# Two pairs of RWKV chunks share one triangular solve, each row on two partitions, all steps on VectorE

## The chip, the cores and the metric

The kernel runs on one core of one Trainium2 chip. A core has TensorE (PE: matmuls and transposes), VectorE (DVE), ScalarE (ACT), GpSimd (POOL) and SyncE (SP, which starts the transfers), each with a queue of its own that it works off in order. The metric is the device time of one execution in microseconds (us); less is better. The time before is 3129.33 us, the median of 3 runs (3124.56 to 3129.62).

## The reference

Two layers (DEPTH = 2) work on 512 latent tokens and 256 context tokens of width 1024. Each layer is a SwiGLU block, a mixer and a second SwiGLU block. The mixer projects its input once, gives a quarter of the width each to attention, RWKV-7 in both directions, pooling and a Fourier transform, and projects the four together back (`w_out`). The change lies in the RWKV part, whose core is a recurrence over time, for 4 heads of 64 and both directions:

```python
def wkv_scan(S0, r, w, k, v, a, b, reverse, emit):
    def step(S, inp):
        r_t, w_t, k_t, v_t, a_t, b_t = inp
        sa = jnp.einsum('bhvk,bhk->bhv', S, a_t)
        S = S * w_t[:, :, None, :] + sa[..., None] * b_t[:, :, None, :] + v_t[..., None] * k_t[:, :, None, :]
        y = jnp.einsum('bhvk,bhk->bhv', S, r_t) if emit else None
        return S, y

    xs = tuple(jnp.moveaxis(t.astype(F32), 1, 0) for t in (r, w, k, v, a, b))
    S_final, ys = lax.scan(step, S0, xs, reverse=reverse)
    return (jnp.moveaxis(ys, 0, 1) if emit else None), S_final
```

The context is scanned first, and its final states are the initial ones of the latent scan. Attention (softmax over 768 keys for the latent tokens) does not depend on the recurrence and is worked off beside it.

## The kernel before

Everything runs under a tile framework: the code names tiles and engines, the framework orders each engine's queue by the order of the code and by priority (`with hot():` lifts what stands in it ahead of other work), and it puts in the waits. Tiles come from pools of fixed size; the solve takes its scratch M and Xs from the pool "w" (11 slots), which also holds the weight tiles.

The recurrence is worked in chunks of 64 tokens. Both directions run at the same time on the two halves of the partitions. There are three groups per mixer: C (the 256 context tokens), L0 (latent, offsets 0 and 256) and L1 (offsets 256 and 0); a group has two pairs of chunks, so a mixer has 12 chunks. Per pair there are three stages:

- `group_pair` scales keys, values and decays (VectorE, GpSimd) into AR and BK, and multiplies them into the chunk's "gram" blocks (line 952, masked at 956). From these comes NTX (line 960), the strictly triangular matrices whose inverses (I + N) are wanted: 32x32 blocks, for 4 heads, 2 directions, 2 chunks and both halves of each chunk, 32 blocks in a pair.
- `group_solve` inverts them. M is the matrix with one block on each partition (line 998 and 1001 transposes, 999 and 1000 copies). X starts as the identity and is worked in 31 steps, j = 31 down to 1, each a multiplication (line 1011) and an addition (line 1013). Each block has four partitions, with 8 of its 32 rows on each. These steps run on GpSimd, except in the first pair of L1 ("late"), where VectorE has them. Behind them stand copies and transposes (1016, 1019, 1020), a product (1030 to 1033) that fills the off-diagonal block (pm1), copies into gram (1042), a second product (1047, pm2) and the last copies (1050). From then on the pair is ready.
- `chain` goes through the pair's two chunks. Each makes z on TensorE (1068, 1071), copies it (Wz, ScalarE, line 1074), multiplies with the inverse (pu, 1077), writes UV (ScalarE 1080 and VectorE 1082), updates the state S (TensorE 1088, VectorE 1090 and 1091), and makes the output y. The next chunk needs the new S.

In the mixer's loop (1470 to 1505) C's pairs and solves come first, in `hot()`. Then both chains of C, each followed by `fill(2)`, which sends out two pieces of attention. Then for each of the four L pairs: `group_pair`, `group_solve`, `fill(2)`, and in `hot()` the chain of the pair before it. What attention is left comes after the loop, `fill(100)`. Layer 0 has 14 pieces of attention, layer 1 nine.

Of the kernel before, what the change touches and what calls it, by code (L numbers as in the profile page):

```python
# [53 lines left out]
class K:  # L54
# [856 lines left out]
    def group_pair(self, R, G, cp):  # L911
# [11 lines left out]
        H = {"G": G, "cp": cp, "gram": [], "A": A, "AR": AR, "late": s == "L" and off[0] and not cp}  # L923
# [63 lines left out]
    def group_solve(self, H):  # L987
# [3 lines left out]
        A = H["A"]  # L991
        X1T, XT, NT = A[0:32], A[32:64], A[64:96]
# [4 lines left out]
        M = w([128, 32, 32], "M")  # L997
        nc.vector.transpose(M[0:32].rearrange(fl), NT.rearrange(fl))
        nc.scalar.copy(M[32:64], M[0:32])
        nc.gpsimd.tensor_copy(M[64:96], M[0:32])  # L1000
        nc.vector.transpose(M[96:128].rearrange(fl), NT.rearrange(fl))
        XS = w([128, 1024], "Xs")
        X, tmp, Pm = XS[:, 0:256].rearrange("p (t i) -> p t i", i=32), XS[:, 256:512], XS[:, 512:768].rearrange("p (u t) -> p u t", t=32)
        nc.gpsimd.memset(XS[:, 0:256], 0.0)
        for x in range(4):
            nc.gpsimd.memset(XS[32 * x:32 * x + 32, x:256:36], 1.0)
        eng = nc.vector if H["late"] else nc.gpsimd
        for j in range(31, 0, -1):
# [18 lines left out]
        for u in range(8):  # L1027
            for d in range(2):
                r = slice(64 * d, 64 * d + 32)
                nc.tensor.matmul(p[r, u], H["gram"][d][r, u, 32:64], X1[d][:, :, 8 * d + u], start=True, stop=True)  # L1030
# [731 lines left out]
```

## Time and profile before

| | value |
|---|---|
| median of 3 runs | 3129.33 us |
| profiled execution | 3129.89 us, span 3128.1 us |
| PE, PEld busy (of the span) | 2910.2 us (93%), 2544.1 us (81%) |
| DVE, ACT, POOL busy | 2303.3 us (74%), 1313.6 us (42%), 531.4 us (17%) |
| chain that ended last | PE 73%, DVE 13%, ACT 7%, POOL 2% |

PE is the time of matmuls, PEld that of weight loads, which overlaps it. The shares are means over the whole span; most of it is SwiGLU, where TensorE is full. The two mixers' recurrences lie at about 780 to 1055 us and 2430 to 2670 us. The chain that ended last is the work followed back from the last instruction, each time to what released it.

### The profile page before, as it was taken

Reading aid. Unit: us, or ns where it says so; the run is one execution under the profiler, and the core shown is the slowest. Engines: PE = TensorE matmul, PEld = TensorE weight load, DVE = VectorE, ACT = ScalarE, POOL = GpSimd, SP = SyncE. Lnnn points to the kernel's source line nnn. Section 1 sums busy time; section 2 is a strip of 40 time slices with the busy share of each in tenths; the row PEclk is TensorE's granted clock in tenths of the full one; section 3 lists DMA queues with packets and bytes.
Section 4 is the critical chain, followed back from the end, with each engine's and each line's share of the span. In section 5 each row is a group of like instructions: output and inputs, shape, how many; then the busy total and the mean of one; then the engine's idle time right before and its main releaser. Section 6 shows DMA issues by size and latency. Waiting matters only on the chain.

```text
span 3128.1 us, 50276 instructions
## 1 busy us (share of the span) xinstructions
PE 2910.2 (93%) x20031; PEld 2544.1 (81%) x20031; DVE 2303.3 (74%) x3989; ACT 1313.6 (42%) x2208; POOL 531.4 (17%) x1117
## 2 busy tenths in 40 slices
PE   7999999999888889999998999999999897879997
PEld 5999998787555679999987999998877565679996
DVE  7879998744666768678778889777834566797887
ACT  4433332433676354333325443332433676354443
POOL 2000002103774030000022000001112764010002
PEclk8999999999686999999999999999999677889998
DMA  6334445320001213233232344434420002033332
GB/s 237 103 116 147 135 140 167 125 66 1 30 28 36 89 60 128 95 108 102 95 122 68 103 141 142 135 122 138 146 67 1 23 29 87 34 111 101 108 109 101
DMA packets 92187, 304.60 MB, mean 97 GB/s; under 512 B 13636, under 2 KB 15920, under 8 KB 91952
## 3 DMA queue, kind: packets, MB, share of 16 engines
q1 hardware_dynamic: 91952, 301.39, 29.2%
q8 instruction: 157, 2.57, 0.3%
q14 instruction: 78, 0.64, 0.1%
HBM read 279.81 MB, written 21.54 MB: 96 GB/s over the span
## 4 chain that ended last, share of the span: by engine, by line
PE 73%; DVE 13%; ACT 7%; issue 3%; DMA 2%; POOL 2%; SPq 0%; DVEq 0%; ACTq 0%; POOLq 0%
PE pab L123 8%; PE pab L124 8%; PE pab L125 8%; PE py L123 6%; PE py L124 6%; PE py L125 6%; PE pgu L123 4%; PE pgu L124 4%; PE pgu L125 4%; PE pw L123 2%; PE pw L124 2%; PE pw L125 2%; DVE wlo L119 2%; DVE raw L420 1%; PE pwo L125 1%
## 5 line engine op out<-in xcount | busy, mean ns | idle before, releaser
L118 ACT CAST whi<-raw 128x1024 fp32r<-128x1024 f32 x488 | 507.8, 1050 | 552.5 <-PE py L125 193.1
L119 DVE TENSOR_TENSOR wlo<-raw,whi 128x1024 fp32r<-128x1024 f32 x488 | 600.6, 1239 | 125.3 <-PE py L124 25.5
L123 PE MATMUL pab<-hshi,whi 128*128 128x256 f32 x1408 | 401.3, 288 | 24.5 <-ACT hshi L118 9.7
L124 PE MATMUL pab<-hslo,whi 128*128 128x256 f32 x1408 | 404.7, 288 | 8.9 <-DVE hslo L119 8.9
L125 PE MATMUL pab<-hshi,wlo 128*128 128x256 f32 x1408 | 401.8, 287 | 1.6 <-DVE wlo L119 1.5
L524 POOL TENSOR_TENSOR acc<-acc,gate 128x512 f32<-128x512 f32 x44 | 73.6, 1695 | 1631.0 <-DMA gate<-gate 1167.1
L123 PE MATMUL pab<-h,whi 128*128 128x256 f32 x1056 | 298.7, 287 | 9.7 <-DVE eab L463 7.4
L124 PE MATMUL pab<-h,whi 128*128 128x256 f32 x1056 | 301.6, 287 | 4.6 <-POOL h L317 4.5
L123 PE MATMUL pgu<-hhiC,whi 128*128 128x256 f32 x1056 | 299.7, 284 | 2.8 <-ACT h L286 2.2
L125 PE MATMUL pab<-h,wlo 128*128 128x256 f32 x1056 | 299.9, 286 | 1.9 <-DVE wlo L119 1.9
L124 PE MATMUL pgu<-hloC,whi 128*128 128x256 f32 x1056 | 299.5, 284 | 0.0
L125 PE MATMUL pgu<-hhiC,wlo 128*128 128x256 f32 x1056 | 299.1, 283 | 0.0
L123 PEld LDWEIGHTS pab<-hshi,whi 128*128 128x128 f32 x1408 | 273.3, 196 | 29.3 <-ACT hshi L118 11.2
L123 PE MATMUL py<-whi,actL 128*128 128x512 f32 x704 | 277.2, 395 | 11.0 <-DVE acc L513 8.3
L124 PEld LDWEIGHTS pab<-hslo,whi 128*128 128x128 f32 x1408 | 275.4, 196 | 11.9 <-DVE hslo L119 11.6
L125 PEld LDWEIGHTS pab<-hshi,wlo 128*128 128x128 f32 x1408 | 274.5, 196 | 3.1 <-DVE wlo L119 2.6
L124 PE MATMUL py<-wlo,actL 128*128 128x512 f32 x704 | 276.8, 393 | 0.0
L125 PE MATMUL py<-whi,actL 128*128 128x512 f32 x704 | 274.8, 391 | 0.0
L123 PEld LDWEIGHTS pab<-h,whi 128*128 128x128 f32 x1056 | 202.8, 194 | 15.9 <-DVE eab L463 8.1
L124 PEld LDWEIGHTS pab<-h,whi 128*128 128x128 f32 x1056 | 205.3, 194 | 9.3 <-POOL h L317 6.3
L125 PEld LDWEIGHTS pab<-h,wlo 128*128 128x128 f32 x1056 | 204.8, 195 | 4.1 <-DVE wlo L119 2.5
L123 PEld LDWEIGHTS pgu<-hhiC,whi 128*128 128x128 f32 x1056 | 202.8, 192 | 6.2 <-ACT h L286 2.7
(473 smaller groups left out, 6586.8 us busy)
## 6 DMA issues: line engine op xcount, KB each, us to landing
raw<-in_w_ffn_in SPq DMA_DIRECT2D x176, 512.0 KB, 3.6
rawm<-in_w_mod SPq DMA_DIRECT2D x128, 512.0 KB, 3.7
raw<-in_w_ffn_out SPq DMA_DIRECT2D x88, 512.0 KB, 3.5
raw<-in_w_in SPq DMA_DIRECT2D x24, 512.0 KB, 4.5
back<-spill SPq DMA_DIRECT2D x44, 256.0 KB, 4.3
spill<-res SPq DMA_DIRECT2D x16, 512.0 KB, 7.3
spill<-acc SPq DMA_DIRECT2D x16, 512.0 KB, 3.3
raw<-in_w_out SPq DMA_DIRECT2D x16, 512.0 KB, 3.5
```

What stands on the lines that cost most here:

```text
L118: self.nc.scalar.copy(hi, src)
L119: self.nc.vector.tensor_tensor(lo, src, hi.bitcast(F32), op=ALU.subtract)
L123: nc.tensor.matmul(out, st[0], mv[0], start=start, stop=False)
L124: nc.tensor.matmul(out, st[0], mv[1], start=False, stop=False)
L125: nc.tensor.matmul(out, st[1], mv[0], start=False, stop=stop)
L420: nc.vector.tensor_tensor(o, x, y, op=ALU.subtract)
L524: nc.gpsimd.tensor_tensor(a[:, sl], a[:, sl], self.gate[s][:, sl], op=ALU.mult)
```

## The change

`group_solve` is called once for a group, with both its pairs. The 64 blocks lie on 128 partitions, two for each block, with 16 of its 32 rows on each. The 31 steps stay, with `(16 - j//2) * j` elements per partition where it was `(8 - j//4) * j`, and their engine is VectorE in all groups. Of M, each pair's part is transposed once (before twice), and two ScalarE copies fill the other half. Copies of X and of gram halve in number and double in length; the products pm1 and pm2 stand for both pairs one behind the other. In the mixer's loop the chains of C move into the loop of L0: after each pair of a group come `fill(2)` and the chain of the group before. The solve stands behind both pairs, and the chains of L1 behind the loop. Four `fill(2)` are left of six; the rest of attention comes with `fill(100)`.

The diff, without the products and the copies into gram (the same for both pairs, in loops over `cp`):

```diff
-    def group_solve(self, H):
-
-
-        nc = self.nc
-        A = H["A"]
-        X1T, XT, NT = A[0:32], A[32:64], A[64:96]
+    def group_solve(self, Hs, eng):
+
+
+        nc = self.nc
-        M = w([128, 32, 32], "M")
-        nc.vector.transpose(M[0:32].rearrange(fl), NT.rearrange(fl))
-        nc.scalar.copy(M[32:64], M[0:32])
-        nc.gpsimd.tensor_copy(M[64:96], M[0:32])
-        nc.vector.transpose(M[96:128].rearrange(fl), NT.rearrange(fl))
+        Ms = [w([128, 32, 32], "M")]
+        M = Ms[0]
+        for cp, H in enumerate(Hs):
+            nc.vector.transpose(M[32 * cp:32 * cp + 32].rearrange(fl), H["A"][64:96].rearrange(fl))
+        nc.scalar.copy(M[64:128, 16:32], M[0:64, 16:32])
+        nc.scalar.copy(M[64:128, 0:16], M[0:64, 0:16])
...
-        X, tmp, Pm = XS[:, 0:256].rearrange("p (t i) -> p t i", i=32), XS[:, 256:512], XS[:, 512:768].rearrange("p (u t) -> p u t", t=32)
-        nc.gpsimd.memset(XS[:, 0:256], 0.0)
-        for x in range(4):
-            nc.gpsimd.memset(XS[32 * x:32 * x + 32, x:256:36], 1.0)
-        eng = nc.vector if H["late"] else nc.gpsimd
+        X, tmp = XS[:, 0:512].rearrange("p (t i) -> p t i", i=32), XS[:, 512:1024]
+        Pm = tmp.rearrange("p (c u t) -> p c u t", c=2, t=32)
+        nc.gpsimd.memset(XS[:, 0:512], 0.0)
+        for y in range(2):
+            nc.gpsimd.memset(XS[64 * y:64 * y + 64, y:512:34], 1.0)
         for j in range(31, 0, -1):
-            a = j // 4
-            tv = tmp[:, 0:(8 - a) * j].rearrange("p (t i) -> p t i", i=j)
-            eng.tensor_tensor(tv, M[:, j:j + 1, 0:j].to_broadcast([128, 8 - a, j]),
-                              X[:, a:8, j:j + 1].to_broadcast([128, 8 - a, j]), op=ALU.mult)
-            eng.tensor_tensor(X[:, a:8, 0:j], X[:, a:8, 0:j], tv, op=ALU.add)
-        for x in range(4):
-            eng = nc.scalar.copy if x % 2 else nc.gpsimd.tensor_copy
-            eng(XT[:, :, x::4], X[32 * x:32 * x + 32].rearrange("p t i -> p i t"))
-        Xb = M[0:32].rearrange("p (x t) u -> p x t u", x=4)
-        for x in range(4):
-            nc.vector.transpose(Xb[:, x].rearrange(fl), X[32 * x:32 * x + 32].rearrange(fl))
-        nc.vector.transpose(X1T.rearrange(fl), XT.rearrange(fl))
-
...
+            a = j // 2
+            tv = tmp[:, 0:(16 - a) * j].rearrange("p (t i) -> p t i", i=j)
+            eng.tensor_tensor(tv, M[:, j:j + 1, 0:j].to_broadcast([128, 16 - a, j]),
+                              X[:, a:16, j:j + 1].to_broadcast([128, 16 - a, j]), op=ALU.mult)
+            eng.tensor_tensor(X[:, a:16, 0:j], X[:, a:16, 0:j], tv, op=ALU.add)
+        Ms.append(w([128, 32, 32], "M"))
+        X1, X2, Xb = [], [], []
+        for cp, H in enumerate(Hs):
+            X1T, XT, X1T2 = [H["A"][32 * i:32 * i + 32] for i in range(3)]
+            Xc = [X[64 * y + 32 * cp:64 * y + 32 * cp + 32] for y in range(2)]
+            nc.gpsimd.tensor_copy(XT[:, :, 0::2], Xc[0].rearrange("p t i -> p i t"))
+            nc.scalar.copy(XT[:, :, 1::2], Xc[1].rearrange("p t i -> p i t"))
+            v = "p (y t) u -> p y t u"
+            Xb.append(Ms[cp][0:32].rearrange(v, y=2))
+            for y in range(2):
+                nc.vector.transpose(Xb[cp][:, y].rearrange(fl), Xc[y].rearrange(fl))
+            nc.vector.transpose(X1T.rearrange(fl), XT.rearrange(fl))
...
             g = self.group_start(P, R, "C", (0, 0), both, first)
             for cp in range(2):
                 Hs.append(self.group_pair(R, g, cp))
-                self.group_solve(Hs[cp])
+            self.group_solve(Hs, nc.vector)
...
-        prev = None
         nth = 0
-        for H in Hs:
-            with hot():
-                self.chain(R, H, False)
-            fill(FILL[l][nth])
-            nth += 1
...
+            prev, Hs = Hs, []
             g = self.group_start(P, R, s, off, em, first)
             for cp in range(2):
-                H = self.group_pair(R, g, cp)
-                self.group_solve(H)
+                Hs.append(self.group_pair(R, g, cp))
                 fill(FILL[l][nth])
                 nth += 1
-                if prev:
-                    with hot():
-                        self.chain(R, prev, False)
-                prev = H
+                with hot():
+                    self.chain(R, prev[cp], False)
+            self.group_solve(Hs, nc.vector)
...
         with hot():
+            self.chain(R, Hs[0], False)
             rw = mixes["L", 1] = self.slot([128, 2, SEQ], name="mixL")[:]
             self.rwkv_out(P, R, "L", rw, (1, 2), "rk")
-            self.chain(R, prev, True)
+            self.chain(R, Hs[1], True)
             self.rwkv_out(P, R, "L", rw, (0, 3), "rk")
         fill(100)
```

On GpSimd the first pair of L0 in layer 0 stood like this before (Xs is X and its scratch, 1011 and 1013 the steps; 1000 a copy of M):

```order
L946 TENSOR_TENSOR AR_8465<-l_r_6263,gb_8193 128x4x64
L1000 COPY M_8287<-M_8287 32x1024
L1011 TENSOR_TENSOR Xs_8292<-M_8287,Xs_8292 128x31
L1013 TENSOR_TENSOR Xs_8292<-Xs_8292 128x31
L1011 TENSOR_TENSOR Xs_8292<-M_8287,Xs_8292 128x30
L1013 TENSOR_TENSOR Xs_8292<-Xs_8292 128x30
L1011 TENSOR_TENSOR Xs_8292<-M_8287,Xs_8292 128x29
```

The new order has, at the same place:

```order
L1004 MEMSET Xs_8260 128x512
L1006 MEMSET Xs_8260 64x16 x2
L1041 MEMSET gram_8059 32x8x32
L965 MEMSET uv_8065 64x512 x2
L935 COPY AR_8529<-l_kk_6262 128x4 x2
L943 TENSOR_TENSOR AR_8529<-l_r_6263,gb_8482 128x4x64
L984 TENSOR_TENSOR kdsL_7745<-kdsL_7745,ga_8481 128x2x256
L1018 COPY NTX_7799<-Xs_8260 32x512
L1018 COPY NTX_8021<-Xs_8260 32x512
```

The 62 steps are gone; two memsets and the copies of X for both pairs (line 1018, before 1016) stand behind each other, with other work of `group_pair` between them.

On VectorE the third chunk of C in layer 0 had its update (line 1082) among attention (1228) and the gram masks (956) before:

```order
L1082 TENSOR_SCALAR uv_7422<-pch_7999 64x256
L1228 ISA pexp_8676,mx_8678<-psc_8680,zero 128x256
L1228 ISA mx_8678 128x1
L956 TENSOR_TENSOR gram_8505<-pgr_8495,prm_858_6192 128x512
L956 TENSOR_TENSOR gram_8505<-pgr_8496,prm_858_6192 128x512
L1228 ISA pexp_8675,mx_8677<-psc_8685,zero 128x512
L1228 ISA mx_8677 128x1
L998 STREAM_TRANSPOSE M_8535<-NTX_8467 32x1024
```

Now the joint solve of L0 stands around it (1010 and 1012 are the steps, 1088 is the update):

```order
L1239 RECIPROCAL mx_8813<-mx_8813 128x1
L1012 TENSOR_TENSOR Xs_8260<-Xs_8260 128x2x29
L1010 TENSOR_TENSOR Xs_8260<-M_8255,Xs_8260 128x56
L1012 TENSOR_TENSOR Xs_8260<-Xs_8260 128x2x28
L1010 TENSOR_TENSOR Xs_8260<-M_8255,Xs_8260 128x81
L1088 TENSOR_SCALAR uv_7282<-pch_8153 64x256
L1012 TENSOR_TENSOR Xs_8260<-Xs_8260 128x3x27
L1010 TENSOR_TENSOR Xs_8260<-M_8255,Xs_8260 128x78
L1012 TENSOR_TENSOR Xs_8260<-Xs_8260 128x3x26
```

What moved: the update of the third chunk comes behind nine steps of L0's solve, and 53 more follow it.

On VectorE the end of L1's second solve in layer 0 was two transposed blocks between other work, and the third chunk of L0 (uv, 1082) came behind it:

```order
L1019 STREAM_TRANSPOSE M_9489<-Xs_9494 32x256 x4
L1147 TENSOR_TENSOR mixC_7845<-mixC_7845,c_r_6257 128x256
L1020 STREAM_TRANSPOSE NTX_9419<-NTX_9419 32x1024
L1148 TENSOR_TENSOR mixC_7845<-mixC_7845,pbon_8930 128x256
L119 TENSOR_TENSOR wlo_10147<-raw_10144,whi_10146 128x1024
L1228 ISA pexp_9687,mx_9689<-psc_9691,zero 128x256
L1228 ISA mx_9689 128x1
L1082 TENSOR_SCALAR uv_8511<-pch_9315 64x256
```

Now the last steps of the joint solve of L1 stand ahead of the transposes of both pairs (1023, 1024), with weight tiles (wlo, 119) and attention (1234) behind them:

```order
L1012 TENSOR_TENSOR Xs_9034<-Xs_9034 128x15x3
L1010 TENSOR_TENSOR Xs_9034<-M_9029,Xs_9034 128x30
L1012 TENSOR_TENSOR Xs_9034<-Xs_9034 128x15x2
L1010 TENSOR_TENSOR Xs_9034<-M_9029,Xs_9034 128x16
L1012 TENSOR_TENSOR Xs_9034<-Xs_9034 128x16
L1239 RECIPROCAL mx_9613<-mx_9613 128x1
L1023 STREAM_TRANSPOSE M_9029<-Xs_9034 32x512 x2
L1023 STREAM_TRANSPOSE M_9100<-Xs_9034 32x512 x2
L1024 STREAM_TRANSPOSE NTX_8531<-NTX_8531 32x1024
L1024 STREAM_TRANSPOSE NTX_8741<-NTX_8741 32x1024
L119 TENSOR_TENSOR wlo_9823<-raw_9820,whi_9822 128x1024
```

All four chunks of L0 have their updates ahead of this place now; the first chunk of L1 has its own 17 rows further on.

## Rows read from the trace of the kernel before

**Rows 1.** Windows: us, busy PE, PEld, DVE, ACT, POOL; PEclk, DMA share, GB/s

```profile
780.00:840.00 60.00, 44.11 (x246) 31.80 (x247) 44.69 (x100) 33.97 (x95) 48.46 (x148) 0.70 0.10 39
840.00:1050.00 210.00, 177.12 (x1867) 128.75 (x1867) 132.63 (x379) 136.82 (x297) 105.03 (x312) 0.74 0.12 41
2490.00:2660.00 170.00, 143.80 (x1568) 105.56 (x1564) 109.64 (x293) 114.68 (x249) 96.77 (x292) 0.74 0.16 56
```

**Rows 2.** Groups by line, 760 to 1060 us: busy us, mean ns, idle before, releaser

```profile
L1013 POOL TENSOR_TENSOR Xs<-Xs 128x66 f32<-128x66 f32 (+22 forms) x155 | 49.9, 330 | 7.0
...
L1019 DVE STREAM_TRANSPOSE M<-Xs 32x256 f32<-32x256 f32 x24 | 10.4, 433 | 1.9 <-POOL Xs L1013 1.2
...
L1011 DVE TENSOR_TENSOR Xs<-M,Xs 128x60 f32<-128x60 f32 (+24 forms) x31 | 8.2, 263 | 0.9
L1013 DVE TENSOR_TENSOR Xs<-Xs 128x60 f32<-128x60 f32 (+24 forms) x31 | 8.1, 262 | 0.9
...
L998 DVE STREAM_TRANSPOSE M<-NTX 32x1024 f32<-32x1024 f32 x6 | 7.4, 1233 | 3.7 <-ACT NTX L960 3.6
```

**Rows 3.** Timeline of ACT, line 1074: start us, duration us, instruction, [idle before <-releaser]

```profile
844.05 0.37 ACT L1074 COPY Wz<-pch 128x256 f32<-128x256 f32 x1 [0.16 <-PE pch L1071]
...
895.80 0.36 ACT L1074 COPY Wz<-pch 128x256 f32<-128x256 f32 x1
945.17 0.37 ACT L1074 COPY Wz<-pch 128x256 f32<-128x256 f32 x1
966.69 0.37 ACT L1074 COPY Wz<-pch 128x256 f32<-128x256 f32 x1 [0.96 <-PE pch L1071]
997.31 0.37 ACT L1074 COPY Wz<-pch 128x256 f32<-128x256 f32 x1
...
1024.67 0.37 ACT L1074 COPY Wz<-pch 128x256 f32<-128x256 f32 x1
...
1048.06 0.37 ACT L1074 COPY Wz<-pch 128x256 f32<-128x256 f32 x1 [5.35 <-PE pch L1071]
...
2541.31 0.37 ACT L1074 COPY Wz<-pch 128x256 f32<-128x256 f32 x1 [1.26 <-PE pch L1071]
2561.80 0.37 ACT L1074 COPY Wz<-pch 128x256 f32<-128x256 f32 x1 [0.95 <-PE pch L1071]
2580.26 0.35 ACT L1074 COPY Wz<-pch 128x256 f32<-128x256 f32 x1
2606.37 0.37 ACT L1074 COPY Wz<-pch 128x256 f32<-128x256 f32 x1
...
2640.33 0.39 ACT L1074 COPY Wz<-pch 128x256 f32<-128x256 f32 x1
...
2667.45 0.37 ACT L1074 COPY Wz<-pch 128x256 f32<-128x256 f32 x1
```

**Rows 4.** Timeline of ACT: the second pair of L0 becomes ready (line 1050)

```profile
978.46 0.74 ACT L1050 COPY gram<-pm 32x256 f32<-32x256 f32 x2
```

**Rows 5.** Timeline of POOL: behind the first solve of C, and L0's last step

```profile
823.12 1.34 POOL L1016 COPY NTX<-Xs 32x256 f32<-32x256 f32 x2
...
946.28 0.21 POOL L1013 TENSOR_TENSOR Xs<-Xs 128x8 f32<-128x8 f32 x1
```

**Rows 6.** Timeline of DVE: the C transposition, and steps of the two late solves

```profile
803.82 1.23 DVE L998 STREAM_TRANSPOSE M<-NTX 32x1024 f32<-32x1024 f32 x1 [0.97 <-ACT NTX L960]
...
935.88 0.17 DVE L1011 TENSOR_TENSOR Xs<-M,Xs 128x31 f32<-128x31 f32 x1
...
968.42 0.37 DVE L1011 TENSOR_TENSOR Xs<-M,Xs 128x49 f32<-128x49 f32 x1
...
972.44 0.17 DVE L1011 TENSOR_TENSOR Xs<-M,Xs 128x8 f32<-128x8 f32 x1
972.65 0.17 DVE L1013 TENSOR_TENSOR Xs<-Xs 128x8 f32<-128x8 f32 x1
...
2611.27 0.21 DVE L1011 TENSOR_TENSOR Xs<-M,Xs 128x49 f32<-128x49 f32 x1
```

More of the change, by code (lines that the diff above doesn't have):

```diff
@@ L922, in group_pair @@
         mul = lambda o, a, b: nc.vector.tensor_tensor(o, a, b, op=ALU.mult)
-        H = {"G": G, "cp": cp, "gram": [], "A": A, "AR": AR, "late": s == "L" and off[0] and not cp}
+        H = {"G": G, "cp": cp, "gram": [], "A": A, "AR": AR}
         for d in range(2):
@@ L1023, in group_solve @@
-        nc.scalar.copy(X1T2[:, :, 8:16], X1T[:, :, 8:16])
-        nc.scalar.copy(M[64:96, :, 24:32], M[0:32, :, 24:32])
-        X1, X2 = (X1T, X1T2), (Xb, Xb2)
-        p = self.ps([128, 8, 32], "pm1", "sv")
-        for u in range(8):
-            for d in range(2):
-                r = slice(64 * d, 64 * d + 32)
-                nc.tensor.matmul(p[r, u], H["gram"][d][r, u, 32:64], X1[d][:, :, 8 * d + u], start=True, stop=True)
-        for d in range(2):
-            r = slice(64 * d, 64 * d + 32)
-            nc.scalar.mul(Pm[r], p[r], -1.0)
@@ L1043, in group_solve @@
-        p = self.ps([128, 8, 32], "pm2", "sv")
-        for u in range(8):
-            for d in range(2):
-                r = slice(64 * d, 64 * d + 32)
-                nc.tensor.matmul(p[r, u].rearrange("p (t x) -> p x t", x=4), Pm[r, u], X2[d][:, :, :, 16 + 8 * d + u], start=True, stop=True)
-        for d in range(2):
-            r = slice(64 * d, 64 * d + 32)
-            nc.scalar.copy(H["gram"][d][r, :, 32:64], p[r])
+        Ms = [w([128, 32, 32], "M")]
+        M = Ms[0]
+        for cp, H in enumerate(Hs):
+            nc.vector.transpose(M[32 * cp:32 * cp + 32].rearrange(fl), H["A"][64:96].rearrange(fl))
@@ new lines, in group_solve @@
+        half = [slice(64 * d, 64 * d + 32) for d in range(2)]
+        p = self.ps([128, 2, 8, 32], "pm1", "sv")
+        for cp, H in enumerate(Hs):
+            for u in range(8):
+                for d, r in enumerate(half):
+                    nc.tensor.matmul(p[r, cp, u], H["gram"][d][r, u, 32:64], X1[cp][d][:, :, 8 * d + u], start=True, stop=True)
+        for r in half:
+            nc.scalar.mul(Pm[r], p[r], -1.0)
+        for cp, H in enumerate(Hs):
+            for d in range(2):
+                gr = H["gram"][d]
+                nc.gpsimd.memset(gr[64 * d + 32:64 * d + 64, :, 0:32], 0.0)
+                for b in range(2):
+                    us = slice(16 * b + 8 * d, 16 * b + 8 * d + 8)
+                    r = slice(64 * d + 32 * b, 64 * d + 32 * b + 32)
+                    for y in range(2):
+                        cpy = nc.gpsimd.tensor_copy if y else nc.scalar.copy
+                        cpy(gr[r, :, 32 * b + y:32 * b + 32:2], Xb[cp][:, y, :, us].rearrange("p t u -> p u t"))
@@ new lines, in group_solve @@
+        p = self.ps([128, 2, 8, 32], "pm2", "sv")
+        for cp in range(2):
+            for u in range(8):
+                for d, r in enumerate(half):
+                    nc.tensor.matmul(p[r, cp, u].rearrange("p (t y) -> p y t", y=2), Pm[r, cp, u], X2[cp][d][:, :, :, 16 + 8 * d + u],
+                                     start=True, stop=True)
+        for cp, H in enumerate(Hs):
+            for d, r in enumerate(half):
+                nc.scalar.copy(H["gram"][d][r, :, 32:64], p[r, cp])
@@ L1469, in mixer @@
         mixes["L", 0] = att["L"]
[L1470 removed]
         nth = 0
[L1472 to L1476 removed]
         for s, off, em in (("L", (0, 256), True), ("L", (256, 0), True)):
[L1478 removed]
+            if off[0] == 0:
                 for n in ("kds", "Y"):
```

15 lines of the change are left out of this document (4 added, 11 removed).

## The prediction

> **What bounds the kernel now.** I read the busy time of each engine in three stretches first [rows 1]. The change touches the two mixers only, and there no engine is full: between 840 and 1050 us TensorE is busy 177.1 of 210 us, VectorE 132.6, ScalarE 136.8 and GpSimd 105.0; in the second layer TensorE has 143.8 of 170. So TensorE leaves 32.9 and 26.2 us idle, and a wait in the recurrence can be worth at most about that. The reader is to see that the stretch before it, 780 to 840, is another case: VectorE is already busy 44.7 of 60 us.
>
> Next I read the lines of the solve [rows 2]. In 760 to 1060 us GpSimd spends 49.9 us on 155 additions (five solves) and about as much on as many multiplications, VectorE 8.2 + 8.1 us on 31 of each (the one "late" solve). A GpSimd step takes 330 ns on average, a VectorE step some 262.
>
> Then I followed the recurrence by the copy that each chunk makes once (Wz, line 1074) [rows 3]. In layer 0 the four chunks of C stand 17.25 us apart on average (844.05 to 895.80). Then 49.4 us pass until the first chunk of L0 (945.17), 21.5 to its second, and 30.6 to its third (997.31). L1 begins at 1024.67 and its four chunks take 23.4 us. In layer 1 the same two waits are 20.5 us (2541.31 to 2561.80) and 26.1 (2580.26 to 2606.37). The third chunk of L0 needs the second pair, whose steps end on GpSimd at 946.28 and whose blocks are written at 978.46 [rows 4, 5]: two solves interleave on one engine there, and 32 us more pass in copies and small matmuls behind them. For the first C pair the way is shorter: steps over at 823.12 [rows 5], Wz at 844.05, 21 us.
>
> **The change part by part.** *The steps.* A joint solve is 31 steps of two operations on (16 - j//2) x j elements per partition, 2856 for each of the two, 5712 in sum. On VectorE with GpSimd idle 49 elements take 0.21 us and 8 take 0.17 [rows 6]: 1.0 ns an element over a base of 0.16, and 0.04 between two steps (972.44, the next at 972.65). So 62 x (0.16 + 0.04) + 5.7 = 18.1 us for a group. While GpSimd runs steps of its own the same 49 elements take 0.37 [rows 6]; 62 x 0.16 more makes 28 us. GpSimd has none of its steps left in the new kernel, so I take the low end, and keep 28 for the range.
>
> The Trainium skill, "SBUF — State Buffer", section "Who interferes with whom", says that VectorE and GpSimd share a pair of ports with an exclusive lock. The two prices in the group just named agree with it. It speaks for this change: it would put the steps at 18.1 us, and only GpSimd's remaining work would add to them.
>
> *VectorE's load.* The steps busy it 62 x 0.16 + 5.7 = 15.6 us a group, 47 a mixer, of which 16.3 was there [rows 2]: +31. Transposes: three of 32x1024 at 1.23 and four of 32x256 at 0.433 per pair become two of 32x1024 and two of 32x512. The last form isn't in the trace; between 0.43 and 1.23 I take 0.70 in proportion to its length. That is 5.4 to 3.9 per pair, -9 us a mixer. Net +22. Of this only about +9 falls into 840 to 1050 (two groups of 15.6, less the old 16.3 and 6 us of transposes): 132.6 becomes 141 of 210, 67%. The C group's 15.6 falls into the stretch where 44.7 of 60 are taken, and nearly fills it. GpSimd loses some 100 us; the copies that it keeps no longer stand behind steps. ScalarE's and GpSimd's strided copies halve in number and double in length; that they cost a few us more or less lies beside other work.
>
> *The C group.* The joint solve needs the second pair, whose block is transposed at 803.82 [rows 6]. 803.8 + 1.2 + 18 to 28 + 21 gives Wz at 844 to 854, before 844.05. I take +5. What hides this is TensorE's other work; if that cover is gone the whole +5 is paid. In the new order the chain of C runs beside the building of L0's pairs. At the old 17.25 us its chunks stand at 849, 866, 884 and 901.
>
> *The L0 group.* On VectorE the solve is queued behind the second C chunk's update, and the third and fourth stand inside it. These are new waits: a chunk late on TensorE holds the rest of the solve, and steps stand before a chunk's update: some 50 of the 62 between the third chunk's and the fourth's, 15 of the 18.1 us, just under the distance of the chunks, which hides them. The last step then comes at about 903; with 21 us behind it L0 begins at 924, before 945.17: -21. With the 32 us of the old second pair it would be 935, -10.
>
> *The L1 group.* Its solve starts behind L0's second chunk (924 + 21.5 = 946) and again has the two others inside: 963, 980, last step 982, L1's first chunk 1003. Before it was 1024.67: -21 holds, and no more comes in, for L0 to L1 takes 79 us as before (79.5). The old wait for the second pair (30.6) becomes a plain 17, and a new one of 23 stands before L1 instead, since both its pairs now become ready at once. By the path layer 0 thus gains 21. TensorE's cap: the 177.1 us of work in 210 can be packed, but not fully; with 8% idle it takes 192.5, a gain of 17.5. I take the smaller, **-17.5**.
>
> *Layer 1.* The first wait was only 20.5 there; 23 in its place is +2.5. L0 to L1 was 78.5 (2561.80 to 2640.33) and becomes 18.5 + 17 + 17 + 23 = 76, -2.5. The path gains nothing at the old distances. But attention moves back in the order. Of its nine pieces in this layer four stood ahead of L0's first pair and eight ahead of L1's; now it is none and four, and one stands behind the last pair. So less TensorE work stands before the solves, and more beside the L1 chain, whose 27.1 us (2640.33 to 2667.45) leave room. The cap with 8% idle is 156.3 for 170: -13.7. Between 0 and that I take **-7**.
>
> *Sum.* The profiled execution took 3129.89 us (span 3128.1), 0.6 above the median of 3129.33. 3129.9 - 17.5 - 7 = 3105.4; **3105** against the median.
>
> **The rivals.** *A, the distances shrink too.* The 17.25 us between chunks is no latency of the chain: L1's four stand 7.8 apart. With both pairs of L0 ready at once, its last two chunks and L1's start could move up by some 5 us each. That is 10 per group and layer in L0 and L1, 40 in all: 3065. For it: TensorE's weight loads fill only 128.8 of 210 us [rows 1]. Against it: attention and the next pairs still stand between these chunks.
>
> The Trainium skill, "Perfetto Trace Analysis", section "Identifying the Most-Contended Engine", calls the busy share of matmuls a bad measure of TensorE's headroom and wants that of weight loads. Here that is 61% against 84%. By it the cap falls away: layer 0 gains 21 instead of 17.5, and rival A is the case.
>
> *B, hidden.* TensorE's idle time has other causes (softmax, copies of ScalarE), and the steps' removal from GpSimd only moves the wait: 3129 within 6.
>
> *C, slower.* A joint solve delays the first pair of each group, and what comes behind the steps is done for both pairs in one piece: transposes, copies, 64 small matmuls. If that takes 32 us, as behind the old second pair, instead of 21, layer 0 has +11 twice on its -21, about 0, and layer 1 +22: 3152. Steps strung out by other VectorE work do the same; the old VectorE solve began at 935.88 and ended at 972.8 [rows 6], 37 us for 16 of work. It decides from the point where L1's last step comes later than about 1004 in layer 0 (1024.67 - 21), and 2619 in layer 1. Against it: GpSimd is free for its half of the copies.
>
> *D, no effect in the queue.* The order might have kept the solves where they were. It hasn't: the steps are gone from GpSimd's queue.
>
> **How the numbers follow.** Forecast 0.46 (3090 to 3120), A 0.18 (3055 to 3080), B 0.15 (3123 to 3135), C 0.21 (3136 to 3155), D none. The range of 8 in 10 leaves out the low half of A and some half of C: 3064 to 3143. The unknown prices lie within: solves at 28 instead of 18 us in L0 and L1 of both layers cost 40 at most, but mostly lie beside chunks that stand inside them. 0.2%, 6 us, is about what a measurement of this kernel tells from no change. Faster by more than that: forecast and A, 0.64; within: 0.15; slower: C, 0.21.
>
> **What would show it.** Steps of 0.17 to 0.25 us on VectorE, 62 for a group in 18 to 25 us of work; no steps on GpSimd. Wz of L0's first chunk near 924, of L1's near 1003; some 20 us from a last step to its group's first Wz; TensorE's idle time down in 840 to 1050. The two mixers differ in their gain, the stretches between them not at all. It would be wrong if VectorE is full from 780 to 840 and C's chain starts at 855 or later, or if the last step of L1 comes after the points above.

## The result: 3090.18 us, and the profile after

The changed kernel takes 3090.18 us in the median (3088.14 to 3093.1, 4 runs), the kernel before 3129.47 in the same comparison: a ratio of 0.9883, 95% interval 0.987 to 0.9897. That is 39 us less, 1.6 times the 24.5 that the sum gave, and at the lower edge of what was held most likely (3090 to 3120). The profiled execution took 3088.14 us, span 3086.3.

First the stages, by windows of the kernel before: layer 0 from the first matmul of the mixer's input projection to the first of its output projection (pw to pwo), the output projection, the SwiGLU blocks between, the next input projection from 4 us behind its start to the second pwo, and that output projection (the 39 us between the third and the fourth are left out). Columns as in [rows 1].

```profile
642.00:1053.60 411.60, 359.76 (x2879) 273.41 (x2877) 238.18 (x619) 222.21 (x484) 175.84 (x480) 0.82 0.11 37
1053.60:1138.60 85.00, 79.16 (x354) 63.70 (x355) 59.40 (x129) 31.85 (x47) 14.54 (x16) 0.96 0.19 69
1138.60:2259.60 1121.00, 1087.92 (x7435) 1010.63 (x7434) 875.23 (x1312) 403.84 (x597) 76.58 (x57) 0.98 0.35 115
2299.00:2668.00 369.00, 320.72 (x2478) 240.60 (x2476) 204.78 (x514) 202.13 (x425) 162.87 (x472) 0.79 0.13 43
2668.00:2730.00 62.00, 53.77 (x249) 41.12 (x249) 40.57 (x92) 17.46 (x24) 5.04 (x5) 0.92 0.08 26
```

The same five stages of the changed kernel:

```profile
641.30:1026.20 384.90, 345.91 (x2854) 263.02 (x2853) 246.80 (x720) 210.73 (x447) 67.57 (x112) 0.84 0.10 34
1026.20:1108.90 82.70, 78.74 (x378) 62.95 (x379) 60.25 (x133) 33.00 (x49) 16.11 (x17) 1.00 0.28 99
1108.90:2225.30 1116.40, 1085.64 (x7435) 1008.98 (x7434) 875.10 (x1312) 404.26 (x597) 76.72 (x57) 0.99 0.35 115
2265.00:2631.70 366.70, 307.21 (x2492) 232.99 (x2490) 224.37 (x621) 191.69 (x388) 59.70 (x105) 0.81 0.12 43
2631.70:2687.60 55.90, 51.71 (x233) 40.11 (x232) 40.04 (x91) 17.41 (x24) 6.09 (x5) 0.95 0.09 29
```

Layer 0 gives 26.7 us up to pwo and 2.3 in it; layer 1 gives 2.3 and 6.1; the blocks between 4.6, though nothing in them was changed. The reader should look at TensorE's two parts. In layer 0 its idle time falls from 51.8 to 39.0 us, and its busy time from 359.8 to 345.9 (25 of some 2870 records fewer lie in that stretch, worth about 3 us at the mean). In layer 1 the idle time *rises* from 48.3 to 59.5, and the busy time falls from 320.7 to 307.2, though 14 matmuls more lie there. Over the whole span the page counts the same 20031 matmuls in both kernels:

```profile
PE 2910.2 (93%) x20031; PEld 2544.1 (81%) x20031; DVE 2303.3 (74%) x3989; ACT 1313.6 (42%) x2208; POOL 531.4 (17%) x1117
```

is the page before, and

```profile
PE 2877.6 (93%) x20031; PEld 2522.9 (82%) x20031; DVE 2332.7 (76%) x4201; ACT 1292.8 (42%) x2136; POOL 322.4 (10%) x383
```

after. Of the 41.8 us of span 32.6 are TensorE's own busy time, 9.2 its idle time. The mean granted clock went from 0.931 to 0.941 of the full 2.4 GHz, and 2910.2 x 0.931 / 0.941 is 2879.3, close to the 2877.6 measured.

The recurrence, by the copy Wz of its chunks as in [rows 3] (the line is 1080 now), with the copies that make L0 ready (1056):

```profile
852.27 0.37 ACT L1080 COPY Wz<-pch 128x256 f32<-128x256 f32 x1
889.84 0.37 ACT L1080 COPY Wz<-pch 128x256 f32<-128x256 f32 x1 [1.43 <-PE pch L1077]
926.38 1.49 ACT L1056 COPY gram<-pm 32x256 f32<-32x256 f32 x4
931.12 0.37 ACT L1080 COPY Wz<-pch 128x256 f32<-128x256 f32 x1
962.13 0.37 ACT L1080 COPY Wz<-pch 128x256 f32<-128x256 f32 x1
998.82 0.36 ACT L1080 COPY Wz<-pch 128x256 f32<-128x256 f32 x1
1024.83 0.37 ACT L1080 COPY Wz<-pch 128x256 f32<-128x256 f32 x1 [1.92 <-PE pch L1077]
...
2464.73 0.37 ACT L1080 COPY Wz<-pch 128x256 f32<-128x256 f32 x1
2533.24 0.37 ACT L1080 COPY Wz<-pch 128x256 f32<-128x256 f32 x1
2600.32 0.37 ACT L1080 COPY Wz<-pch 128x256 f32<-128x256 f32 x1
2628.05 0.37 ACT L1080 COPY Wz<-pch 128x256 f32<-128x256 f32 x1 [0.75 <-PE pch L1077]
```

These are the first and last chunk of each group in layer 0, and in layer 1 the first of each group and the last of all. L0 begins at 931.12 instead of 945.17, L1 at 998.82 instead of 1024.67, and the last chunk comes at 1024.83 instead of 1048.06. C's chunks stand 12.5 us apart (17.25 before), L0's 10.3.

The solves in windows from first to last step: C, L0 and L1 of layer 0. Columns as above.

```profile
799.50:827.30 27.80, 25.34 (x112) 18.48 (x112) 23.07 (x102) 14.26 (x42) 0.19 (x1) 0.88 0.20 78
874.20:898.10 23.90, 19.70 (x168) 14.87 (x166) 20.48 (x75) 14.11 (x29) 2.23 (x2) 0.71 0.01 2
946.10:975.10 29.00, 24.23 (x303) 16.22 (x301) 25.60 (x105) 19.15 (x43) 0.00 (x0) 0.99 0.00 1
```

The same windows, only VectorE's instructions on the tile Xs (columns: us, VectorE busy and count, clock, DMA share, GB/s):

```profile
799.50:827.30 27.80, 15.71 (x62) 0.88 0.20 78
874.20:898.10 23.90, 16.38 (x63) 0.71 0.01 2
946.10:975.10 29.00, 15.67 (x62) 0.99 0.00 1
```

The 62 steps take 15.7 us in C and L1, as worked out, and 16.4 in L0 (the 63rd instruction there is a transposition). But a solve lasts 24 to 29 us in layer 0, and 24, 32 and 31 in layer 1: in its stretch in layer 0 VectorE is busy 83 to 88%, with 4 to 10 us of other work between the steps. The steps' own work follows what GpSimd does meanwhile: over the six solves it is 15.7 to 15.8 us where GpSimd is busy up to 0.2 us, 16.4 and 16.8 where it is busy 2.2 and 2.4, and 18.2 where it is busy 4.8 (the second of layer 1). Such a place in L0, VectorE's timeline, where two updates of the state (1096, 1097) stand among steps:

```profile
880.97 0.29 DVE L1010 TENSOR_TENSOR Xs<-M,Xs 128x126 f32<-128x126 f32 x1
881.64 0.87 DVE L1096 TENSOR_TENSOR S<-prm,pch 64x256 f32<-64x256 f32 x2 [0.38 <-PE pch L1094]
882.54 0.29 DVE L1012 TENSOR_TENSOR Xs<-Xs 128x126 f32<-128x126 f32 x1
882.75 0.86 DVE L1097 TENSOR_TENSOR S<-S,PC 64x256 f32<-64x256 f32 x2
```

### The profile page after: what moved, and what is told of

Its sections match the earlier page's. It is cut to its first block, busy times and chain, and to the rows that moved or that the text cites. A ratio compares the mean times of both kernels' runs of the same rounds, so it can differ in the third digit from the quotient of the medians.

```text
span 3086.3 us, 49684 instructions
## 1 busy us (share of the span) xinstructions
PE 2877.6 (93%) x20031; PEld 2522.9 (82%) x20031; DVE 2332.7 (76%) x4201; ACT 1292.8 (42%) x2136; POOL 322.4 (10%) x383
## 5 line engine op out<-in xcount | busy, mean ns | idle before, releaser
L118 ACT CAST whi<-raw 128x1024 fp32r<-128x1024 f32 x488 | 507.9, 1050 | 535.7 <-PE py L125 177.2
L123 PE MATMUL pab<-hshi,whi 128*128 128x256 f32 x1408 | 400.8, 288 | 25.4 <-ACT hshi L118 10.3
L123 PEld LDWEIGHTS pab<-hshi,whi 128*128 128x128 f32 x1408 | 272.7, 195 | 30.0 <-ACT hshi L118 11.6
L124 PEld LDWEIGHTS pab<-hslo,whi 128*128 128x128 f32 x1408 | 275.2, 196 | 11.9 <-DVE hslo L119 11.6
```

What stands on the lines that cost most here:

```text
L118: self.nc.scalar.copy(hi, src)
L123: nc.tensor.matmul(out, st[0], mv[0], start=start, stop=False)
L124: nc.tensor.matmul(out, st[0], mv[1], start=False, stop=False)
```

## The experiments

Theory S says that the shorter solve (on VectorE, half as many steps) gives the gain, rival O that the order does: C's chain beside the building of L0's pairs. Four kernels take these apart; eight more test single terms. For each run two stretches of its profiled execution stand here in us, worked out from the first and last start of the matmuls: layer 0 from the first pw to the last pwo, and layer 1 from the last matmul of the context's SwiGLU (py) to the last pwo. A stretch is that of one execution, and executions of one kernel lie 4 to 15 us apart (joint solves on GpSimd: 3101.9 to 3116.9), so small differences between stretches tell nothing.

| kernel | median | layer 0 | layer 1 |
|---|---|---|---|
| before | 3126 to 3129 | 496.6 | 470.3 |
| changed | 3090.2 | 467.6 | 462.3 |
| new loop, old solves | 3110.5 | 479.7 | 469.0 |
| old loop, separate solves on VectorE | 3112.7 | 488.9 | 464.3 |
| new loop, separate solves on VectorE | 3114.1 | 487.9 | 465.1 |
| joint solves on GpSimd | 3110.3 | 474.0 | 470.1 |
| C's chain ahead | 3122.4 | 480.9 | 479.8 |
| half the steps | 3072.1 | 457.7 | 454.6 |
| multiplications twice | 3165.0 | 508.5 | 495.3 |
| C's solve on GpSimd | 3110.1 | 482.2 | 467.8 |
| context's output among L0 | 3101.5 | 470.5 | 469.0 |
| context's output in L1's chain | 3106.2 | 472.3 | 475.4 |
| three pieces of attention | 3110.3 | 480.1 | 464.2 |
| latent solves ahead | 3092.6 | 468.4 | 461.5 |

### The new loop with the old solves

```diff
-            self.group_solve(Hs, nc.vector)
+            for H in Hs:
+                self.solve1(H, nc.vector if off[0] and not H["cp"] else nc.gpsimd)
```

`solve1` is the old `group_solve`; in C its engine is `nc.gpsimd`.

> The changed kernel's loop (C's chains inside L0's loop, four fills, both pairs built before a group's solves), but each pair solved by itself as before: four partitions a row, 62 steps a pair on GpSimd, the first pair of L1 on VectorE. Theory S (the shorter solve gives the gain): nothing is gained, since two GpSimd solves now stand behind both pairs: 3125 to 3145 us. Rival O (the order gives it: C's chain beside the building of L0's pairs, attention further back): most of the 39 us stays, 3092 to 3105.

Measured: 3110.48 us, ratio 0.9945 (0.9929 to 0.9961). Neither: the order alone gives some 15 us, nearly all in layer 0, not nothing and not most.

### The old loop, all twelve solves on VectorE

```diff
-        eng = nc.vector if H["late"] else nc.gpsimd
+        eng = nc.vector
```

> The kernel before with one word changed: all twelve separate solves on VectorE, its loop untouched. Theory S in its engine form (steps of 0.2 us instead of 0.33, no contention): L0's second pair no longer shares GpSimd with the first, so the 49 and 30 us waits of layer 0 shrink, 3100 to 3115 us. Rival O: VectorE takes over 12 solves of 15 us, the order has the same waits, 3122 to 3140.

Measured: 3112.74 us, 0.9955 (0.994 to 0.997), within what S expected. VectorE is nearly full while L0's two solves run on it, from the first step to the last of the second pair:

```profile
873.30:938.90 65.60, 55.71 (x493) 39.92 (x490) 60.93 (x262) 45.37 (x92) 20.00 (x44) 0.81 0.06 20
```

60.9 of 65.6 us. The engine alone is worth 13 us.

### The new loop, separate solves on VectorE

```diff
-            self.group_solve(Hs, nc.vector)
+            for H in Hs:
+                self.solve1(H, nc.vector)
```

> The changed kernel's loop, each pair solved by itself on VectorE, one after the other: 124 steps of about 0.2 us a group instead of 62, some 28 us instead of 18. Packing form of S (half as many steps): each of the six groups waits up to 10 us longer, of which the four L groups count: 3105 to 3130 us. Engine form and rival O: 3088 to 3100, because the first pair is ready after 14 us, before the joint solve would be.

Measured: 3114.12 us, 0.9957 (0.9942 to 0.9972): the packing form. The order and the engine together are worth no more than either alone. L0's 124 steps take 63 us here, where the joint 62 take 24, and VectorE has 61.1 of these 63.2 us:

```profile
877.20:940.40 63.20, 50.38 (x390) 35.72 (x388) 61.14 (x259) 45.17 (x87) 19.19 (x40) 0.90 0.10 34
```

The packing, half the steps and half the copies, is worth 24 us on top of the other two. That VectorE is full in that stretch is the likely reason; it was not tried apart.

### The joint solves on GpSimd

```diff
-            self.group_solve(Hs, nc.vector)
+            self.group_solve(Hs, nc.gpsimd)
```

> The changed kernel with its 62 joint steps of a group on GpSimd instead of VectorE, nothing else. Engine form of S: a GpSimd step takes 0.33 us for about 50 elements and more for the joint tile's 92 on average, so a joint solve takes 22 to 30 us instead of 18, alone on its engine; 5 to 10 us more at each of the L groups: 3100 to 3120 us. Packing form and rival O: 3085 to 3098, for VectorE is rid of 47 us a mixer.

Measured: 3110.27 us (3101.94 to 3116.94), 0.9955 (0.9938 to 0.9971): the engine form. The steps by line in L0's stretch, on GpSimd (busy us, mean ns):

```profile
L1012 POOL TENSOR_TENSOR Xs<-Xs 128x126 f32<-128x126 f32 (+22 forms) x31 | 12.8, 414 | 2.1
L1010 POOL TENSOR_TENSOR Xs<-M,Xs 128x126 f32<-128x126 f32 (+22 forms) x31 | 11.3, 364 | 6.0 <-ACT M L999 3.8
```

24.1 us of steps, 35 us from first to last, 11 more than on VectorE. Layer 0 ends 6 us later, layer 1 8. TensorE's busy time is 2871.9 us at a mean clock of 0.944, less than in the changed kernel, but its idle time is 19 us longer. So a high clock alone does not make the time. The profiled execution was the fastest of the four, 8 us under their median. That the steps' price on GpSimd is what this run pays is not shown; the run with C's solve alone on GpSimd, below, speaks against it.

### C's chain ahead of the loop

```diff
+        for H in Hs:
+            with hot():
+                self.chain(R, H, False)
+            fill(FILL[l][nth])
+            nth += 1
...
-                with hot():
-                    self.chain(R, prev[cp], False)
+                if off[0]:
+                    with hot():
+                        self.chain(R, prev[cp], False)
```

> The changed kernel with C's two chains where they stood before: ahead of the loop over the L groups, each followed by two pieces of attention, so that L0's pairs are built behind them; joint solves on VectorE as they are. If bringing C's chain beside the building of L0's pairs is what the order gives, L0's first chunk comes 15 to 25 us later than 931 in layer 0 and the time is 3100 to 3120 us. If the joint solve on VectorE gives the gain wherever C's chain stands: 3086 to 3096.

Measured: 3122.36 us (3113.54 to 3125.42, 10 runs), 0.9983 (0.9972 to 0.9994). L0's first chunk comes at 943.5, 12 us later than in the changed kernel, less than expected, but the time is even a little above what was expected for the order. With C's chain where it was, the joint solve on VectorE is worth some 4 us; with the chain moved, 20 on top of the move. The run is not clean, since it also puts four more pieces of attention ahead of and among the pairs, which the run with three pieces below shows to cost something in layer 0.

### Half the steps

```diff
-        for j in range(31, 0, -1):
+        for j in range(31, 0, -2):
```

> The changed kernel with every second of the 31 steps left out (j = 31, 29, ... 1), so that its X is not the inverse; all else is done. A joint solve has 32 operations instead of 62, about 9 us less. If the steps are on the path that sets the end in all L groups, four times 9, or six with C's: 3036 to 3058 us. If they lie mostly beside TensorE's work (the cap of the prediction): 3070 to 3088.

Measured: 3072.09 us, 0.9829 (0.9814 to 0.9844), 18 us under the changed kernel. The steps of all six solves keep VectorE busy 52.2 us instead of 98.6, 46 less (the expected 54 counts the gaps between steps): mostly hidden. L1's last chunk comes at 1004.8, 20 us earlier, but layer 0 ends only 10 earlier. What was gained in the chain is half given back behind it.

### The multiplications twice

```diff
             eng.tensor_tensor(tv, M[:, j:j + 1, 0:j].to_broadcast([128, 16 - a, j]),
                               X[:, a:16, j:j + 1].to_broadcast([128, 16 - a, j]), op=ALU.mult)
+            eng.tensor_tensor(tv, M[:, j:j + 1, 0:j].to_broadcast([128, 16 - a, j]),
+                              X[:, a:16, j:j + 1].to_broadcast([128, 16 - a, j]), op=ALU.mult)
```

> The changed kernel with each of the 31 multiplications issued twice (the second writes the same values), so that a joint solve has 93 operations on VectorE instead of 62, about 9 us more. With half the steps the time fell by 18 us for 54 us less of work, a third. If that third is the price of a step on the path, +18 here: 3103 to 3114 us. If VectorE becomes the bound (rival C of the prediction): each of the 54 us counts, 3130 to 3150. If the third was only the order that changed: 3085 to 3097.

Measured: 3164.97 us, 1.0122 (1.0104 to 1.014), 75 us over the changed kernel. The steps of all six solves keep VectorE busy 147.9 us instead of 98.6, 49 more. More than each microsecond counts. L0's solve in this kernel, all engines and then Xs on VectorE:

```profile
893.60:935.80 42.20, 31.65 (x249) 22.49 (x248) 38.00 (x144) 22.08 (x47) 4.36 (x6) 0.72 0.00 1
...
893.60:935.80 42.20, 26.15 (x93) 0.72 0.00 1
```

The 93 steps are 26 us of the 42; VectorE is busy 90%, and 12 us of other work stand between. This solve grows by 18 us, not by 9, for more of that work stands in it; the six together grow by 65. C's first chunk moves from 852 to 871, L0's to 961, L1's to 1036. So the changed kernel seems to stand at a knee: some 0.4 us back for each that the steps lose, 1.5 to pay for each that they gain. With one run on each side, and TensorE's order changed in several hundred rows of each layer in both, that is a reading and not a measured slope. Rival C of the prediction is there, 8 us of steps a solve further on.

### C's solve on GpSimd

```diff
                 Hs.append(self.group_pair(R, g, cp))
-            self.group_solve(Hs, nc.vector)
+            self.group_solve(Hs, nc.gpsimd)
         F = self.qk_prep(P, z, streams, last)
```

> The changed kernel with C's joint solve on GpSimd and the two L groups' on VectorE. In the run with all joint solves on GpSimd C's chain began at 853.4 in layer 0, as in the changed kernel (852.3). Theory: C's solve costs nothing on either engine, VectorE's other work between 780 and 840 us comes 15 us earlier: 3080 to 3090 us. Rival: GpSimd's slower steps delay C's chain in layer 1 (there 9 us later relative to the start), 3090 to 3102.

Measured: 3110.1 us, 0.9954 (0.9938 to 0.9969), 20 worse, beyond both. C's chain comes at 858 instead of 852 (2 of the 6 us already at the mixer's start). L0's solve, still on VectorE, begins 8 us later and lasts 41 us instead of 24, and layer 0 takes 15 longer:

```profile
882.60:923.70 41.10, 36.41 (x292) 24.43 (x292) 37.27 (x148) 26.03 (x54) 6.07 (x7) 0.88 0.00 1
```

148 instructions instead of 75. By line, among them are twelve row maxima of attention, which the changed kernel has none of in this stretch:

```profile
L1234 DVE CUSTOM_DVE_ANT_0 pexp<-psc,zero 128x256 f32<-128x256 f32 (+1 forms) x12 | 6.5, 555 | 0.1
```

The framework has ordered VectorE anew, and put attention and the context's output among the steps. This run also bears on the one with all joint solves on GpSimd: 3110.27 us there, 3110.1 here. Once C's solve is on GpSimd, the engine of the two L groups makes no difference to the median, so the 20 us of that run can't be put down to dearer steps in the L groups.

### The context's output elsewhere

In both runs the block behind L0's solve goes:

```diff
-            if s == "L" and off[0] == 0 and both:
-                with hot():
-                    self.rwkv_out(P, R, "C", mixes["C"][:, 1], (0, 1), "ch")
```

In the first it comes into the loop of L1, in the second between the chains of L1's pairs:

```diff
                     self.chain(R, prev[cp], False)
+                if off[0] and cp == 0 and both:
+                    with hot():
+                        self.rwkv_out(P, R, "C", mixes["C"][:, 1], (0, 1), "ch")
```

```diff
             self.chain(R, Hs[0], False)
+            if both:
+                self.rwkv_out(P, R, "C", mixes["C"][:, 1], (0, 1), "ch")
```

In the changed kernel L0 of layer 0 waits 33 us from the last step (897.9) to its first chunk. TensorE's timeline there (pm is the solve's products, pyT and pbon the context's output):

```profile
916.51 0.87 PE L1052 MATMUL pm<-M,Xs 32*32 32x32 f32 x22
920.03 0.48 PE L1150 MATMUL pyT<-ident,kdsYC 128*128 128x128 f32 x1 [2.64 <-DVE kdsYC L1138]
920.92 0.47 PE L1150 MATMUL pyT<-ident,kdsYC 128*128 128x128 f32 x1 [0.41 <-DVE kdsYC L1138]
921.18 1.06 PE L1145 MATMUL pbon<-kdsYC,prm 128*128 128x256 f32 x2
922.17 1.22 PE L1146 MATMUL pbon<-hida,prm 64*128 64x256 f32 x2
923.32 0.86 PE L1052 MATMUL pm<-M,Xs 32*32 32x32 f32 x22
```

> The changed kernel with the context's group norm and output (rwkv_out of C, layer 0 only) moved from behind L0's solve to behind the first two chunks of L0. In the changed kernel its transposes stand in TensorE's queue in the middle of L0's second product and wait for VectorE and GpSimd. Theory: that wait is why L0's way from the last step to the first chunk took 33 us, where the other five took 18 to 25; it falls to 20 to 25, L0's first chunk moves up by 8 to 12, and the time is 3078 to 3086 us. Rival: TensorE's work is only put elsewhere in the layer, 3087 to 3093.

Measured: 3101.48 us, 0.9925 (0.991 to 0.994).

> As the run before, with the context's output still later, between the second and the third chunk of L1. Theory: L0's way from last step to first chunk falls to 20 to 25 us here too, but the output's work now stands in the last chain, where it delays the end by some of its 6 us: 3080 to 3090 us. Rival: no gain, 3087 to 3096.

Measured: 3106.24 us, 0.9936 (0.9917 to 0.9955). In both the first chunk of L0 comes 6 us earlier, at 925.48 and 924.87:

```profile
925.48 0.37 ACT L1080 COPY Wz<-pch 128x256 f32<-128x256 f32 x1
```

The way is 28 us, so the output's blocks were about 5 of the 8 to 12 in question. But the work is only put elsewhere: layer 0 ends 3 and 5 us later than in the changed kernel. Layer 1, which has no such output, takes 7 and 13 us longer. Its code is the same; the orders of the two kernels differ from the changed kernel's there by some 150 of TensorE's rows. No theory or rival had times as long as these; the rival was right that the work is only put elsewhere, and moreover an edit in one layer reorders the other. That the 7 and 13 us come from that order is not shown: these are single executions, and the second kernel's lie between 3098 and 3111.

### Three pieces of attention, and the latent solves ahead

```diff
-FILL = ((2,) * 6, (2,) * 6)
+FILL = ((3,) * 6, (3,) * 6)
```

> The changed kernel with three pieces of attention after each pair instead of two, so that twelve stand among the pairs, as many as before. The prediction gave 7 us of layer 1 to attention that moves back. If so, 3094 to 3104 us. If the framework's order follows what is ready more than the place in the code: 3086 to 3094.

Measured: 3110.28 us (3104.91 to 3118.31), 0.9945 (0.9929 to 0.9962). Attention further ahead does cost, 20 us, more than expected, but nearly all of it in layer 0: layer 1 takes 464.2 us against 462.3. Up to L0's last chunk layer 0 agrees within 0.5 us; then L1 begins 5 us later, and the output projection takes 90.9 us instead of 82.7:

```profile
1030.70:1121.60 90.90, 83.99 (x396) 66.01 (x396) 59.96 (x132) 32.85 (x49) 18.92 (x17) 0.94 0.20 74
```

at a clock of 0.94 where the changed kernel has 1.00, the upper of the two levels.

```diff
-            self.group_solve(Hs, nc.vector)
+            with hot():
+                self.group_solve(Hs, nc.vector)
             if s == "L" and off[0] == 0 and both:
```

> The changed kernel with the solves of the L groups lifted ahead of other work like the chains. The order changes little (some 20 rows of TensorE, 30 of VectorE). If the steps' other company on VectorE is what stretches a solve to 24 to 31 us, 3 to 8 us less: 3080 to 3087. If the order is already that: 3087 to 3093; anything beyond would be what a few moved rows do by themselves.

Measured: 3092.57 us, 0.9891 (0.9874 to 0.9908): the same as the changed kernel, and the order was already that.

None of the orders or engines tried beats the changed kernel; only the run that leaves out steps is below it. But the runs that move the context's output or bring attention forward leave steps, engine and packing as they are, and cost 11 to 20 us all the same. So what order, engine and packing are worth one by one, differences of 4 to 24 us, is not told apart from what a new order of the queues does by itself.

## Why the prediction held, and where its steps failed

**The steps' price** held: 15.6 us of work predicted, 15.7 to 16.4 measured in layer 0. So did the sum for VectorE's load, +22 us a mixer: from the first pw to the end of the output projection of layer 0 its steps rise from 16.3 to 47.8 us and its transpositions fall from 32.6 to 23.1. Yet its busy time rose by only 8.6 up to pwo (238.2 to 246.8), and by 19.6 in layer 1. The difference lies mostly in its other work, which the sum took as fixed: the 642 instructions that both kernels have there beside the solve took 282.9 us before and 272.9 after, and the 502 of layer 1 223.1 and 220.3. Two of layer 0, in the Fourier part, give 3.8 of these 10 us. GpSimd's steps no longer run beside them; that this is the reason was not tried apart.

**The length of a solve** was mis-sized: 18.1 us were predicted, with 28 for steps under contention. It was 24 to 29 in layer 0, and not by contention: the steps' work was at most 0.7 us above 15.7 there, and 2.5 in layer 1. The term that was missing is VectorE's other work in the same queue, 4 to 10 us a solve. The share of VectorE in 840 to 1050 (67% predicted) hid that it is 83 to 88% just where the steps stand.

**C's first chunk** came at 852.3, predicted 849. The sign of being wrong that stands at 855, with VectorE full from 780 to 840, did not show: VectorE was busy 50.9 of those 60 us.

**The distances between chunks** are the step that failed in my disfavour. "At the old 17.25 us" was 12.5 in C and 10.3 in L0. Rival A named this and asked for 5 us at some of the chunks; in C alone it was 4.7 at each, in L0 more. It was given 0.18. Against it I had set that attention and the next pairs still stand between chunks; they do, and the chunks are closer nevertheless.

**The way from last step to first chunk** was 21 us in the sum, 32 in rival C. Measured in layer 0: 25.0 for C, 33.0 for L0, 23.7 for L1. So rival C's term was there once. It and the longer solves ate what the distances gave: from a group's last chunk to the next group's first, where the sum had 23 us each time (901 to 924, 980 to 1003), it took 41.3 (889.84 to 931.12) and 36.7 (962.13 to 998.82). So L0 came at 931 (924 predicted), L1 at 999 (1003), the last chunk at 1024.8 (1026.4, 1003 and the old 23.4). The path of layer 0, -21 in the text, was -23. That near agreement comes from two errors against each other.

**TensorE's cap** was the wrong step of the sum. It took the 177.1 us of busy time as fixed and let only idle time go, which gave -17.5 for layer 0. Half of layer 0's gain is busy time (359.8 to 345.9). And the idle time fell by less than those 17.5: before (780 to 840, then to the first pwo)

```profile
780.00:840.00 60.00, 44.11 (x246) 31.80 (x247) 44.69 (x100) 33.97 (x95) 48.46 (x148) 0.70 0.10 39
840.00:1053.60 213.60, 180.26 (x1895) 130.53 (x1894) 135.15 (x386) 139.62 (x300) 105.56 (x313) 0.74 0.12 41
```

and after

```profile
780.00:840.00 60.00, 49.68 (x232) 35.52 (x232) 50.88 (x159) 37.74 (x102) 13.44 (x29) 0.73 0.11 39
840.00:1026.20 186.20, 160.52 (x1883) 116.40 (x1883) 136.58 (x423) 125.23 (x259) 31.20 (x61) 0.78 0.10 34
```

From 840 on it is 33.3 and 25.7 us, 7.7 less; another 5.6 went between 780 and 840 (15.9 to 10.3), where the sum had no gain. So the sum came near with a term whose make-up was wrong.

That the busy time goes by the granted clock is shown by all fourteen kernels. The table's stretch of layer 0 has 3231 matmuls in each of them, that of layer 1 2925. Their busy time times the mean granted clock over just the busy times gives nearly the same everywhere, 375 to 381 us in layer 0 and 338 to 344 in layer 1. Before it is 439.0 us at 0.854 and 411.6 at 0.827, after 424.6 at 0.886 and 396.5 at 0.852. So some 30 of the 42 us that the span lost are the same matmuls at a higher clock. What raised the clock is not shown, for no run changed it by itself, and whether it came from the shorter recurrence stays open. In 20 us windows of both kernels, 780 to 800 and 840 to 860, it reads, before:

```profile
780.00:800.00 20.00, 8.39 (x34) 5.09 (x35) 19.38 (x36) 3.38 (x6) 17.32 (x39) 0.52 0.02 5
...
840.00:860.00 20.00, 19.32 (x176) 14.73 (x176) 9.92 (x28) 14.97 (x39) 9.55 (x30) 0.52 0.01 2
```

and after:

```profile
780.00:800.00 20.00, 15.01 (x59) 10.77 (x59) 18.50 (x40) 11.62 (x33) 4.45 (x12) 0.66 0.06 14
...
840.00:860.00 20.00, 20.00 (x243) 15.88 (x244) 11.54 (x32) 13.99 (x34) 3.39 (x8) 0.71 0.01 2
```

In both windows the clock was near the lower level (1.2 GHz is 0.50) before, and TensorE had been idle 11.6 of the 20 us in the first; with 5 idle it was 0.66. In the window 840 to 860 TensorE did 243 matmuls at 0.71 where it did 176 at 0.52, busy nearly all the time in both, though not the same matmuls.

The Trainium skill, "Perfetto Trace Analysis", section "Identifying the Most-Contended Engine", had spoken against that cap, by the share of weight loads. This trace agrees that matmul busy time is no measure of the room, though by the clock: it shrank by 32.6 us. But the weight loads shrank too (2544.1 to 2522.9), so their share is no fixed amount of work either.

**Layer 1**: -7 predicted, 8.4 measured up to the end of its output projection. The size held, by luck, for the reason did not. Idle time did not fall but rose by 11 up to the second pwo, by 7 with the output projection; the gain is busy time, 15.6 us less, at a higher clock (0.79 to 0.81, then 0.92 to 0.95). The path did not stay as it was either: from L0's first chunk to L1's it took 67.1 us (2533.24 to 2600.32), where 78.5 stood before and 76 were predicted. And three pieces of attention after each pair, which put all nine of this layer ahead again, left layer 1 where it was (464.2 us, 462.3 with two).

**"The stretches between them not at all"**: the SwiGLU blocks took 4.6 us less, 1121.0 to 1116.4, at a mean clock of 0.98 and 0.99. In the other runs this stretch lay between 1115 and 1119.5; why it is longest in the kernel before stays open.

**Rivals.** A holds in its mechanism, for the distances shrank, but not in its size: it asked for 40 us beyond the forecast, and the time is 15 beyond it; the waits before L0 and L1 took back much of what the distances gave. B falls. C's two mechanisms are both there, a 33 us way once and strung-out steps everywhere, but below the point that was given: the last step of L1 was over at 975.1, before 1004, and in layer 1 at 2582.8, before 2619. The run with doubled multiplications passes it (1018) and is slower than before. The order, the engine and the packing give 39 us only together; the order alone, the engine alone and the three pairs of them gave 4 to 15, and the packing alone was not run.

## What to carry to other kernels

What a chain of small instructions costs is read from its own stretch: its work plus the other work queued between on that engine. Where that engine was full here, halving the count on top of the other two changes was worth 24 us, and the faster engine alone 13. Where TensorE's clock is below its upper level, its busy time is not a fixed load to pack: here it fell with the clock's rise, in layer 1 even while the idle time rose, so a cap on idle time was no upper bound. And under a scheduling framework a small edit reorders places far away; edits that changed none of the work cost 11 to 20 us here. So variants should be compared stage by stage, and a difference of that size is not yet the price of what was edited.

## What the runs showed that was not expected

The slope is not the same on both sides: 46 us less of steps in six solves gave 18 us, 49 us more cost 75. L0's joint steps take 264 ns on VectorE on average and 389 on GpSimd. And with C's solve on GpSimd, whose chain begins within 1 to 6 us of the same time on either engine, L0's solve on VectorE lasted 41 us instead of 24, in another order of the queue. TensorE's busy time in the mixers, times its granted clock, is the same within 2% in all fourteen kernels.
